# Gate and up products of a mixture-of-experts layer: two quarters of weights per change between fp32r and bf16 products

## The chip, the cores and the metric

The kernel runs on one core of a Trainium2 chip. The metric is the device time of one execution in microseconds (us). TensorE appears in the profile as PE (matmuls) and PEld (weight loads), VectorE as DVE, ScalarE as ACT, GpSimd as POOL and the DMA queue that loads weights as SP.

## The reference, cut to what matters

One encoder layer is applied to 512 prompt tokens and 1024 sample tokens. The part that the change touches is the expert layer: each of 16 experts takes its best 64 prompt and 128 sample tokens, 192 columns in all.

```python
def expert_choice_moe(h, w_router, w_gate, w_up, w_down):
    ...
    gates, idx = lax.top_k(probs.T, cap)
    xe = jnp.take(t, idx, axis=0)
    a = jnp.einsum("ecd,edf->ecf", xe, w_gate)
    b = jnp.einsum("ecd,edf->ecf", xe, w_up)
    ye = jnp.einsum("ecf,efd->ecd", jax.nn.silu(a) * b, w_down)
    ye = ye * gates[..., None].astype(ye.dtype)
    out = jnp.zeros_like(t).at[idx.reshape(-1)].add(ye.reshape(-1, D))
```

The widths are 1024 for a token, 2048 for an expert's inner layer. All arrays are fp32.

## The kernel before, in words

Every fp32 weight is used as a sum of a rounded fp32r part (`wh`, made by ACT in `split_hi`, L937) and a bf16 remainder (`wl`, made by DVE in `split_lo`, L946). Tokens too are kept as a high part, its remainder and a bf16 copy.

The weights of an expert come in six units of 4 MB: gate and up of the first half of the inner layer, gate and up of the second half, and two halves of down. Each unit is worked in four quarters; `QS` lists all quarters in order and `qi` counts them. A quarter of gate or up is 256 inner columns, that is two blocks of 128 (`f`) by eight blocks of depth (`k`). One expert therefore has 16 quarters of gate and up (4 g, 4 u, 4 g, 4 u) and 8 of down.

`gu_mm` (L1172) does one quarter on PE: 16 fp32r products of 384 columns (L1180, the tokens and their remainder side by side), and then 16 bf16 products of 192 columns (L1184), which add the weights' remainder to the first 192 columns. Both sum into one PSUM tile `pg`. The pool `psG` has two buffers of it, which are four of the eight PSUM banks; `S` and `Pp` of the down products hold the other four.

`gu_out` (L1238) takes the tile out of PSUM: ACT copies the remainder's columns into `t` (L1243) and DVE adds the others to it (L1244), and after that `pg` is free. A gate quarter then gets a sigmoid on ACT (L1250) and a product on DVE into `sil` (L1251). An up quarter gets a product with `sil` on DVE (L1255) and is split into the operand `hT` of the down products: two ACT copies (L1263, L1266) and two DVE subtractions (L1264, L1265). `t` and `sg` have two buffers each (pool `ev`).

Every engine runs its own instructions in the order in which they are written, and waits by semaphores for the others. The order is written out in the loop over `qi`: the products of quarter `qi` come first, then `gu_out` of the quarter before it, and inside that, at the call `between()`, the weight splits for later quarters: `split_hi(qi + 3)` on ACT and `split_lo(qi + 2)` on DVE. `wh` has four buffers and `wl` six. When the last quarter of a unit is split, `load` issues the DMA of the unit after the next into the raw buffer that came free (two buffers).

Of the kernel before, what the change touches and what calls it, by code (L numbers as in the profile page):

```python
# [6 lines left out]
F32 = mybir.dt.float32  # L7
F32R = mybir.dt.float32r
BF16 = mybir.dt.bfloat16
I32 = mybir.dt.int32  # L10
U32 = mybir.dt.uint32
AF = mybir.ActivationFunctionType
# [5 lines left out]
P = 128  # L18
D = 1024
KD = D // P  # L20
# [6 lines left out]
KF = FE // P  # L27
# [8 lines left out]
def encoder(ctx: ExitStack, tc, xp, xs_, pp, ps_, norm1_g, w_in, conv_k, conv_b, ln_g, ln_b, pool_w,  # L36
            pool_scale, w_out, norm2_g, w_router, w_gate, w_up, w_down, w_ple, w_pg, b_pg, final_g,
            yp, ys):
    nc = tc.nc
# [28 lines left out]
    def rpool(name, bufs, st=None):  # L68
        return (st or rgt).enter_context(tc.tile_pool(name=name, bufs=bufs, side="right"))
# [11 lines left out]
    for g in range(4):  # L81
        h = 1 << g
# [674 lines left out]
    def own(e):  # L757

        return (0, CP, 0) if e % 2 == 0 else (CP, 0, CS)
# [51 lines left out]
    for it in range(24):  # L811
        b, r = divmod(it, 8)
        c, h = divmod(r, 2)
# [93 lines left out]
    NQ = len(QS)  # L907
    RAW, HL = {}, {}

    def load(u, pieces=range(4)):  # L910
        if u >= NU:
            return
        down = units[u][1:3] == ("d", NE - 1)
        if 0 in pieces:
            RAW[u] = rawp.tile([P, KF, 512] if down else [P, KD, D], F32, name="raw")
        step = 4 if down else 2
        src = units[u][0].rearrange("(k p) n -> p k n", p=P)
        for q in pieces:
            c = slice(q * step, (q + 1) * step)
            nc.sync.dma_start(RAW[u][:, c, :], src[:, c, :])  # L920

    def split_hi(qi):
        if qi >= NQ:
            return
        u, q = QS[qi]
        raw = RAW[u]
        if units[u][1] in "gu":
            src = raw[:, :, q * 256:(q + 1) * 256]
            shape = [P, KD, 256]
        elif units[u][1:3] == ("d", NE - 1):  # L930
            src = raw[:, 4 * q:4 * q + 4, :]
            shape = [P, 4, 512]
        else:
            src = raw[:, 2 * q:2 * q + 2, :]
            shape = [P, 2, D]
        h = hlp.tile(shape, F32R, name="wh")
        nc.scalar.activation(h, src, AF.Copy)  # L937
        HL[qi] = (h, src, shape)

    def split_lo(qi):  # L940
        if qi >= NQ:
            return
        u, q = QS[qi]
        h, src, shape = HL[qi]
        l = hlp2.tile(shape, BF16, name="wl")
        nc.vector.tensor_sub(l, src, h.bitcast(F32))  # L946
        HL[qi] = (h, l)
        if q == 3:
            RAW.pop(u)
            load(u + 2)  # L950
# [115 lines left out]
    for i in range(12):  # L1066
        a = 4 * i
        at(a + 1, x1_half, i, 0)
        at(a + 3, x1_half, i, 1)
        t = max(a + 2, OB + 2 * i)  # L1070
# [91 lines left out]
    with ExitStack() as sc:  # L1162
        hep = rpool("he", 1, sc)
        ev = rpool("ev", 2, sc)
        ev1 = rpool("ev1", 1, sc)
        ps_g = sc.enter_context(tc.tile_pool(name="psG", bufs=2, space=PSUM))
        ps_d = sc.enter_context(tc.tile_pool(name="psD", bufs=1, space=PSUM))

        hT = None
        sil = None  # L1170
        S = Pp = None

        def gu_mm(e, qi):
            h, l = HL.pop(qi)
            xT, xb = XT[e]
            pg = ps_g.tile([P, 2, 512], F32, name="pg")
            c = slice(own(e)[0], own(e)[0] + 192)
            for f in range(2):
                for k in range(KD):
                    nc.tensor.matmul(pg[:, f, 0:384].rearrange("p (a t) -> p a t", a=2), h[:, k, f * P:(f + 1) * P],  # L1180
                                     xT[:, k, :, c], start=(k == 0), stop=False)
            for f in range(2):
                for k in range(KD):
                    nc.tensor.matmul(pg[:, f, 0:192], l[:, k, f * P:(f + 1) * P], xb[:, k, c],  # L1184
                                     start=False, stop=(k == KD - 1))
            return pg

        WL = []

# [44 lines left out]
                                             start=False, stop=True, skip_group_check=True)  # L1234
                WL.clear()

        LA = 3
        def gu_out(kind, e, hf, q, pg, between):  # L1238

            nonlocal hT, sil  # L1240
            f0 = 8 * hf + 2 * q
            t = ev.tile([P, 2, 192], F32, name="t")
            nc.scalar.activation(t, pg[:, :, 192:384], AF.Copy)  # L1243
            nc.vector.tensor_add(t, pg[:, :, 0:192], t)  # L1244
            sg = ev.tile([P, 2, 192], F32, name="sg")
            if kind == "g":
                between()
                if q == 0:
                    sil = ev1.tile([P, KD, 192], F32, name="sil")
                nc.scalar.activation(sg, t, AF.Sigmoid)  # L1250
                nc.vector.tensor_mul(sil[:, 2 * q:2 * q + 2, :], t, sg)  # L1251
            else:
                if hf == 0 and q == 0:
                    hT = (hep.tile([P, KF, 384], F32R, name="hT"), hep.tile([P, KF, 192], BF16, name="hTb"))
                nc.vector.tensor_mul(sg, t, sil[:, 2 * q:2 * q + 2, :])  # L1255
                last = hf == 1 and q == 3
                if not last:
                    between()
                hh = hT[0][:, f0:f0 + 2, :]

                _, so, po = own(e)
                a, b = (64, 0) if e % 2 == 0 else (0, 192)
                nc.scalar.activation(hh[:, :, a:a + 192], sg, AF.Copy)  # L1263
                nc.vector.tensor_sub(hh[:, :, 256:384], sg[:, :, so:so + CS], hh[:, :, a + so:a + so + CS].bitcast(F32))  # L1264
                nc.vector.tensor_sub(hh[:, :, b:b + CP], sg[:, :, po:po + CP], hh[:, :, a + po:a + po + CP].bitcast(F32))  # L1265
                nc.scalar.activation(hT[1][:, f0:f0 + 2, :], sg, AF.Copy)  # L1266
                if last:
                    between()

        YT = []  # L1270

        def down_out(e, hf, q, between):

            between()
            if q < 3 or hf == 0 and e < NE - 1:
                return
            if hf == 0 or e < NE - 1:
                YE[0] = ev1.tile([P, D], F32, name="ye_s")
                YE[1] = ev1.tile([CP, D], F32, name="ye_p")
            cs = (0, 1) if e < NE - 1 else (hf,)  # L1280
            for n in cs:
                nc.scalar.activation(YE[0][:, n * 512:(n + 1) * 512], S[:, n, :], AF.Copy, scale=gt_s[:, e:e + 1])  # L1282
            for n in cs:
                t = ev1.tile([CP, 512], F32, name="yt")
                nc.scalar.activation(t, Pp[CP:, n, :], AF.Copy, scale=gt_p[CP:, e:e + 1])
                nc.vector.scalar_tensor_tensor(YE[1][:, n * 512:(n + 1) * 512], Pp[:CP, n, :], gt_p[:CP, e:e + 1], t,  # L1286
                                               op0=OP.mult, op1=OP.add)
            c = slice(cs[0] * 512, (cs[-1] + 1) * 512)
            for g, src, ix in (("s", YE[0], idx_s[:, e:e + 1]), ("p", YE[1], idx_p[:CP, e:e + 1])):
                nc.gpsimd.indirect_dma_start(out=acc_d[g], out_offset=bass.IndirectOffsetOnAxis(ap=ix, axis=0),  # L1290
                                             in_=src[:, c], in_offset=None, element_offset=c.start,
                                             compute_op=OP.add)

        YE = {}
        late = None
        for qi in range(NQ - 4):
            u, q = QS[qi]
            _, kind, e, hf = units[u]
            nxt = None
            between = lambda: (split_hi(qi + LA), split_lo(qi + LA - 1)) if qi < NQ - 5 else None  # L1300
            if kind == "d" and hf == 0 and q == 0:
                late(between)
                late = None
            if kind in "gu":
                pg = gu_mm(e, qi)
                nxt = lambda f, a=(kind, e, hf, q, pg): gu_out(*a, f)
            elif kind == "d":
                if qi == NQ - 5:
                    pt = ps_g.tile([P, 2, 512], F32, name="pg")
                    pt = pt.rearrange("p i (k t) -> p i k t", k=4)  # L1310
                    for f in (t_T, t_split):
                        for i in range(2):
                            f(i, 0, pt[:, i])
                down_mm(e, hf, q, qi)
                nxt = lambda f, a=(e, hf, q): down_out(*a, f)
            if late:
                late(between)
            elif not (kind == "d" and hf == 0 and q == 0):
                between()
            late = nxt  # L1320
            if qi == NQ - 6:
                rx = rawp.tile([P, KF, 512], F32, name="raw")
                for i in range(2):
                    x2_load(i, slice(0, 512))
            if kind == "d" and 1 <= 4 * hf + q <= 4:
                turn(e + 1, 4 * hf + q - 1, lambda: ps_g.tile([P, 2, 512], F32, name="pg"))
# [10 lines left out]
    with ExitStack() as sd:  # L1337
# [58 lines left out]
        for i in range(12):  # L1396
# [5 lines left out]
            for n in range(len(cuts) - 1):  # L1402
                c = slice(cuts[n], cuts[n + 1])
# [57 lines left out]
```

## Time and profile before

| | us |
|---|---|
| median of 3 runs (lowest to highest) | 2303.33 (2302.74 to 2307.52) |
| the profiled execution, its time | 2308.3 |
| its span, first to last instruction | 2306.5 |

The profile describes that one execution. Besides busy times it gives, for each group of instructions, the idle time of the engine just before them and the instruction that ended it. A chain view follows the work that ended last back through time, and a timeline shows each engine's instructions with start and length; runs of equal instructions are merged as x16 and the like. The ends of matmuls are modelled, and a matmul's length includes its way through the array, so that consecutive ones overlap: what counts is the distance of their starts.

### The profile page before, as it was taken

The page shows a single profiled execution, that of the slowest core. Times are in us where ns is not written, and L with a number is a line of the kernel's source. Part 1 is how long each engine was busy: PE and PEld are TensorE (multiplying, and loading weights), DVE is VectorE, ACT ScalarE, POOL GpSimd, SP SyncE. Part 2 cuts the span into 40 slices and gives each one's busy share as a digit, 9 for nine tenths or more (in the row PEclk, how much of TensorE's full clock was granted, in tenths as well). Part 3 has the DMA queues.
Part 4 walks back from the last instruction along what each step waited for, and adds up shares of the span by engine and source line. Part 5 has one row for each costly group of instructions (what it writes and reads, how often), then busy time and mean ns, then how long its engine had stood idle before and what let it go on. Part 6 is the DMA issues. An engine that isn't in the chain of part 4 may idle for free.

```text
span 2306.5 us, 36990 instructions
## 1 busy us (share of the span) xinstructions
PE 2243.6 (97%) x15062; PEld 1912.3 (83%) x15106; DVE 1734.4 (75%) x2320; ACT 1404.2 (61%) x1837; POOL 277.0 (12%) x538
## 2 busy tenths in 40 slices
PE   7999889988999999999999999999999999999997
PEld 6888777768898979889798988979788898988675
DVE  8898763576877878787787878778787877878565
ACT  4324336546767667676676767667676766666443
POOL 0122232221001010100101010010101001000322
PEclk9999999999999999999999999999999999999999
DMA  6434555547687686767767676876767677777442
GB/s 194 109 118 122 165 163 174 196 169 289 246 292 259 254 293 245 282 243 296 253 259 285 254 280 243 297 246 261 282 262 271 251 292 246 273 249 272 144 138 101
DMA packets 168874, 534.26 MB, mean 232 GB/s; under 512 B 11969, under 2 KB 38625, under 8 KB 168704
## 3 DMA queue, kind: packets, MB, share of 16 engines
q1 hardware_dynamic: 156064, 493.70, 58.5%
q0 software_dynamic: 9040, 31.46, 5.5%
q10 hardware_dynamic: 3600, 6.74, 0.8%
q8 instruction: 118, 1.93, 0.3%
q14 instruction: 52, 0.43, 0.1%
HBM read 481.34 MB, written 50.52 MB: 231 GB/s over the span
## 4 chain that ended last, share of the span: by engine, by line
PE 78%; issue 10%; DMA 4%; DVE 4%; ACT 2%; POOL 1%; SPq 0%; ACTq 0%; DVEq 0%; POOLq 0%
PE pg L1180 27%; PE pg L1184 13%; PE S L1217 9%; PE Pp L1217 4%; PE S L1227 4%; PE Pp L1233 2%; PE pz L103 2%; PE pz L104 2%; PE pz L105 2%; PE po L1369 2%; PE po L1370 2%; PE po L1372 2%; PE pz L413 2%; DMA acc_s<-ye_s,idx_s 1%; PE pz L606 1%
## 5 line engine op out<-in xcount | busy, mean ns | idle before, releaser
L946 DVE TENSOR_TENSOR wl<-raw,wh 128x2048 bf16<-128x2048 f32 x388 | 881.7, 2283 | 65.6 <-issue 54.9
L1180 PE MATMUL pg<-xTe,wh 128*128 128x384 f32 x4096 | 777.3, 341 | 2.7 <-ACT wp L997 2.7
L937 ACT ACTIVATE wh<-raw 128x2048 fp32r<-128x2048 f32 x388 | 736.1, 1909 | 38.4 <-DMA raw<-in_w_up_dram 20.2
L1180 PEld LDWEIGHTS pg<-xTe,wh 128*128 128x128 f32 x4096 | 701.5, 188 | 9.3 <-ACT ye_s L1282 6.2
L1184 PE MATMUL pg<-xTb,wl 128*128 128x192 bf16 x4096 | 382.8, 247 | 0.0
L1184 PEld LDWEIGHTS <-wl 128*128 128x128 bf16 x4096 | 325.2, 98 | 40.3 <-issue 40.3
L1243 ACT ACTIVATE t<-pg 128x384 f32<-128x384 f32 x256 | 125.9, 492 | 300.4 <-PE pg L1184 299.7
L1217 PE MATMUL S<-wh,hT 128*128 128x512 f32 x1024 | 285.4, 398 | 0.6 <-ACT ye_s L1282 0.6
L1244 DVE TENSOR_TENSOR t<-pg,t 128x384 f32<-128x384 f32 x256 | 142.7, 557 | 158.7 <-ACT t L1243 157.9
L1217 PEld LDWEIGHTS S<-wh,hT 128*128 128x128 f32 x1024 | 186.4, 188 | 36.7 <-ACT ye_s L1282 1.0
L103 PE MATMUL pz<-xTh,wb 128*128 128x256 f32 x576 | 167.0, 290 | 0.7 <-ACT xTh L212 0.5
L104 PE MATMUL pz<-xTl,wb 128*128 128x256 f32 x576 | 164.4, 285 | 1.5 <-DVE xTl L213 1.5
L105 PE MATMUL pz<-xTh,wb 128*128 128x256 f32 x576 | 164.2, 285 | 0.0
L746 POOL DMA_INDIRECT xg_s<-h_s,idx_s x16 | 24.2, 1513 | 1159.1 <-PE pg L778 579.1
L1217 PE MATMUL Pp<-wh,hT 128*128 128x512 f32 x512 | 160.9, 390 | 0.8 <-DVE ye_p L1286 0.8
L429 DVE SCALAR_TENSOR_TENSOR acc<-u,kT,acc 128x496 f32<-128x496 f32 (+2 forms) x168 | 126.8, 755 | 5.1
L103 PEld LDWEIGHTS pz<-xTh,wb 128*128 128x128 f32 x576 | 111.8, 194 | 10.8 <-issue 5.8
L1217 PEld LDWEIGHTS Pp<-wh,hT 128*128 128x128 f32 x512 | 96.1, 188 | 22.3 <-DVE ye_p L1286 1.2
L782 DVE SCALAR_TENSOR_TENSOR xTe<-pg,vT,xTe 128x128 fp32r<-128x128 f32 (+1 forms) x120 | 49.5, 412 | 86.0 <-ACT xTe L781 83.9
L104 PEld LDWEIGHTS pz<-xTl,wb 128*128 128x128 f32 x576 | 111.9, 194 | 1.9 <-DVE xTl L213 1.7
L105 PEld LDWEIGHTS pz<-xTh,wb 128*128 128x128 f32 x576 | 111.9, 194 | 0.0
L1227 PE MATMUL S<-wl,hTb 128*128 128x512 bf16 x480 | 108.8, 379 | 2.2
(290 smaller groups left out, 2661.0 us busy)
## 6 DMA issues: line engine op xcount, KB each, us to landing
raw<-in_w_gate_dram SPq DMA_DIRECT2D x128, 1024.0 KB, 6.4
raw<-in_w_up_dram SPq DMA_DIRECT2D x128, 1024.0 KB, 8.4
raw<-in_w_down_dram SPq DMA_DIRECT2D x128, 1024.0 KB, 6.3
u<-u_d SPq DMA_DIRECT2D x32, 262.0 KB, 5.5
st<-yT_d SPq DMA_DIRECT2D x12, 512.0 KB, 5.6
ple_d<-wp SPq DMA_DIRECT2D x12, 512.0 KB, 8.9
pl<-ple_d SPq DMA_DIRECT2D x12, 512.0 KB, 4.7
out_dram<-raw SPq DMA_DIRECT2D x11, 512.0 KB, 2.9
```

Of the source, the lines that this page charges most:

```text
L103: nc.tensor.matmul(out, wh, xh, start=first, stop=False)
L104: nc.tensor.matmul(out, wh, xl, start=False, stop=False)
L105: nc.tensor.matmul(out, wl, xh, start=False, stop=last)
L429: nc.vector.scalar_tensor_tensor(acc[:, :n], u[:, s:s + n], kT[:, c, s:s + 1], acc[:, :n], op0=OP.mult, op1=OP.add)
L937: nc.scalar.activation(h, src, AF.Copy)
L946: nc.vector.tensor_sub(l, src, h.bitcast(F32))
L1180: nc.tensor.matmul(pg[:, f, 0:384].rearrange("p (a t) -> p a t", a=2), h[:, k, f * P:(f + 1) * P], xT[:, k, :, c], start=(k == 0), stop=False)
L1184: nc.tensor.matmul(pg[:, f, 0:192], l[:, k, f * P:(f + 1) * P], xb[:, k, c], start=False, stop=(k == KD - 1))
L1217: nc.tensor.matmul(out[:, n, :], x, rhs(h, i, n), start=(k == 0 and first), stop=(out is Pp and k == KF - 1))
L1227: nc.tensor.matmul(S[:, n, :], hT[1][:, k, so:so + CS], rhs(l, i, n), start=False, stop=(k == KF - 1))
L1243: nc.scalar.activation(t, pg[:, :, 192:384], AF.Copy)
L1244: nc.vector.tensor_add(t, pg[:, :, 0:192], t)
```

## The change

Gate and up are worked in pairs of quarters. `gu_mm` takes two `pg` tiles, does the 32 fp32r products of both quarters and then the 32 bf16 products of both. `gu_out` evicts both tiles, and does the rest for both, with one call of `between()` in the pair. The splits are handed out by two counters (`NXT`) instead of fixed offsets: at a gate or up pair that begins at quarter `qi`, both kinds are brought up to quarter `qi + 3`, that is two of each; down quarters do as before. The pools are as before, so a pair takes both `pg` buffers, both `t` and both `sg`.

```diff
         def gu_mm(e, qi):
-            h, l = HL.pop(qi)
+            hl = [HL.pop(qi + i) for i in range(2)]
             xT, xb = XT[e]
-            pg = ps_g.tile([P, 2, 512], F32, name="pg")
+            pgs = [ps_g.tile([P, 2, 512], F32, name="pg") for _ in range(2)]
...
+            for pg, (h, _) in zip(pgs, hl):
+                for f in range(2):
+                    for k in range(KD):
+                        nc.tensor.matmul(pg[:, f, 0:384].rearrange("p (a t) -> p a t", a=2),
+                                         h[:, k, f * P:(f + 1) * P], xT[:, k, :, c], start=(k == 0), stop=False)
+            for pg, (_, l) in zip(pgs, hl):
+                for f in range(2):
+                    for k in range(KD):
+                        nc.tensor.matmul(pg[:, f, 0:192], l[:, k, f * P:(f + 1) * P], xb[:, k, c],
+                                         start=False, stop=(k == KD - 1))
+            return pgs
...
-        def gu_out(kind, e, hf, q, pg, between):
+        def gu_out(kind, e, hf, q, pgs, between):
...
+            ts = []
+            for pg in pgs:
+                t = ev.tile([P, 2, 192], F32, name="t")
+                nc.scalar.activation(t, pg[:, :, 192:384], AF.Copy)
+                nc.vector.tensor_add(t, pg[:, :, 0:192], t)
+                ts.append(t)
+            sgs = [ev.tile([P, 2, 192], F32, name="sg") for _ in range(2)]
             if kind == "g":
                 between()
...
+                for i in range(2):
+                    nc.scalar.activation(sgs[i], ts[i], AF.Sigmoid)
+                    nc.vector.tensor_mul(sil[:, 2 * (q + i):2 * (q + i) + 2, :], ts[i], sgs[i])
+                return
...
+            for i in range(2):
+                nc.vector.tensor_mul(sgs[i], ts[i], sil[:, 2 * (q + i):2 * (q + i) + 2, :])
+            last = hf == 1 and q == 2
+            if not last:
+                between()
...
+        NXT = {"hi": 3, "lo": 2}
+        def splits(hi, lo):
+            for key, f, n in (("hi", split_hi, hi), ("lo", split_lo, lo)):
+                while NXT[key] <= min(n, NQ - 3 - (key == "lo")):
+                    f(NXT[key])
+                    NXT[key] += 1
+
         for qi in range(NQ - 4):
...
+            if kind in "gu" and q % 2:
+                continue
             nxt = None
-            between = lambda: (split_hi(qi + LA), split_lo(qi + LA - 1)) if qi < NQ - 5 else None
+            z = qi + (kind in "gu")
+            between = lambda: splits(z + 3 - (kind in "gu"), z + 2) if qi < NQ - 5 else None
```

On PE, at the first two changes of quarters of expert 0, the order before is this; `wl` is the bf16 remainder of the weights, and the 16 loads and products of a quarter are cut after the first.

```order
L1180 MATMUL pg<-xTe,wh 128x384 x16
L1184 LDWEIGHTS wl
L1184 MATMUL pg<-xTb,wl 128x192
...
L1180 MATMUL pg<-xTe,wh 128x384 [waits DVE_49]
L1180 MATMUL pg<-xTe,wh 128x384 x15
L1184 LDWEIGHTS wl
```

At the same place of the changed kernel, the beginning of the second pair, it is this.

```order
L1187 MATMUL pg<-xTb,wl 128x192
L1182 MATMUL pg<-xTe,wh 128x384 [waits DVE_49]
L1182 MATMUL pg<-xTe,wh 128x384 x15
L1182 MATMUL pg<-xTe,wh 128x384 [waits DVE_49]
L1182 MATMUL pg<-xTe,wh 128x384 x15
L1187 LDWEIGHTS wl
```

The wait for DVE's addition of an older tile stands ahead of each tile's first product in both; the tile waited for was the one before last, with a whole quarter of products behind it, and is now the first of the pair just ended.

On DVE, in gate quarters and then an up quarter of an expert, the order before is this: addition, a weight split, product, quarter by quarter.

```order
L1244 TENSOR_TENSOR t<-pg,t 128x384 [waits Activation_49]
L946 TENSOR_TENSOR wl<-raw,wh 128x2048
L1251 TENSOR_TENSOR sil<-t,sg 128x384 [waits Activation_49]
L1244 TENSOR_TENSOR t<-pg,t 128x384 [waits Activation_49]
L1255 TENSOR_TENSOR sg<-t,sil 128x384 [waits DVE_49]
L946 TENSOR_TENSOR wl<-raw,wh 128x2048
L1264 TENSOR_TENSOR hT<-sg,hT 128x2x128 [waits DMASW7_49,DMASW2_49,Activation_49]
L1265 TENSOR_TENSOR hT<-sg,hT 128x2x64
```

In the changed kernel the same stretch, the second gate pair and an up pair, is this.

```order
L1247 TENSOR_TENSOR t<-pg,t 128x384 [waits Activation_49] x2
L946 TENSOR_TENSOR wl<-raw,wh 128x2048 [waits Activation_49] x2
L1256 TENSOR_TENSOR sil<-t,sg 128x384 [waits Activation_49] x2
L1247 TENSOR_TENSOR t<-pg,t 128x384 [waits Activation_49] x2
L1261 TENSOR_TENSOR sg<-t,sil 128x384 [waits DVE_49] x2
L946 TENSOR_TENSOR wl<-raw,wh 128x2048 [waits Activation_49] x2
L1272 TENSOR_TENSOR hT<-sg,hT 128x2x128 [waits Activation_49]
L1273 TENSOR_TENSOR hT<-sg,hT 128x2x64
```

The remainder splits `wl` now wait for ACT, which they did not before: the high part that they need is made in the same pair and not one quarter earlier.

On ACT, in the same gate quarters, the order before is the first of the next two pieces, and that of the changed kernel the second.

```order
L1243 ACTIVATE t<-pg 128x384 [waits PE_49,Activation_49]
L937 ACTIVATE wh<-raw 128x2048
L1250 ACTIVATE sg<-t 128x384 [waits DVE_49]
L1243 ACTIVATE t<-pg 128x384 [waits PE_49,Activation_49]
L937 ACTIVATE wh<-raw 128x2048
```

```order
L1246 ACTIVATE t<-pg 128x384 [waits DVE_49,PE_49] x2
L937 ACTIVATE wh<-raw 128x2048 x2
L1255 ACTIVATE sg<-t 128x384 [waits DVE_49] x2
L1246 ACTIVATE t<-pg 128x384 [waits DVE_49,PE_49] x2
L937 ACTIVATE wh<-raw 128x2048 [waits DMAHW2_49,DMAHW7_49,DMAHW1_49,DMAHW0_49]
L937 ACTIVATE wh<-raw 128x2048
```

The first copy of a pair out of PSUM now waits for DVE as well as for PE: it writes into the buffer `t` that the product of the gate pair before it reads.

## Rows read from the trace of the kernel before

**Rows 1.** The page: the span, and PE's busy time with its share.

```profile
span 2306.5 us, 36990 instructions
PE 2243.6 (97%) x15062; PEld 1912.3 (83%) x15106; DVE 1734.4 (75%) x2320; ACT 1404.2 (61%) x1837; POOL 277.0 (12%) x538
```

**Rows 2.** The chain that ended last, one gate quarter: start, us, what.

```profile
1158.14 2.81 PE pg L1180 x16
1160.95 1.33 PE pg L1184 x16
```

**Rows 3.** Windows: length, busy PE, PEld, DVE, ACT, POOL, PEclk, DMA.

```profile
1170.58:1203.75 33.17, 33.17 (x257) 31.91 (x257) 28.32 (x33) 23.41 (x28) 0.00 (x0) 1.00 0.67 254
2130.00:2150.00 20.00, 17.45 (x86) 11.44 (x85) 8.82 (x6) 7.68 (x9) 6.61 (x2) 1.00 0.56 179
```

**Rows 4.** Timelines of PE alone, short windows in one gate quarter: start, length.

```profile
1191.10 0.60 PE L1180 MATMUL pg<-xTe,wh 128*128 128x384 f32 x2
...
1193.96 1.50 PE L1184 MATMUL pg<-xTb,wl 128*128 128x192 bf16 x16
```

**Rows 5.** The page's groups: busy us, mean ns of one, idle before.

```profile
L1184 PE MATMUL pg<-xTb,wl 128*128 128x192 bf16 x4096 | 382.8, 247 | 0.0
...
L1243 ACT ACTIVATE t<-pg 128x384 f32<-128x384 f32 x256 | 125.9, 492 | 300.4 <-PE pg L1184 299.7
```

**Rows 6.** Timeline, an eviction in a gate quarter and one among up quarters.

```profile
1195.24 3.03 PE L1180 MATMUL pg<-xTe,wh 128*128 128x384 f32 x16
1195.56 0.49 ACT L1243 ACTIVATE t<-pg 128x384 f32<-128x384 f32 x1 [1.44 <-PE pg L1184]
1195.94 1.91 ACT L937 ACTIVATE wh<-raw 128x2048 fp32r<-128x2048 f32 x1
1196.08 0.56 DVE L1244 TENSOR_TENSOR t<-pg,t 128x384 f32<-128x384 f32 x1 [0.92 <-ACT t L1243]
...
1198.75 0.55 DVE L1251 TENSOR_TENSOR sil<-t,sg 128x384 f32<-128x384 f32 x1
...
1203.50 0.42 DVE L1264 TENSOR_TENSOR hT<-sg,hT 128x256 fp32r<-128x256 f32 x1
...
1203.83 0.28 DVE L1265 TENSOR_TENSOR hT<-sg,hT 128x128 fp32r<-128x128 f32 x1
...
1206.40 1.50 PE L1184 MATMUL pg<-xTb,wl 128*128 128x192 bf16 x16
...
1207.94 0.49 ACT L1243 ACTIVATE t<-pg 128x384 f32<-128x384 f32 x1 [0.97 <-PE pg L1184]
```

**Rows 7.** Timelines of ACT and DVE, splits back to back.

```profile
1214.64 3.70 ACT L937 ACTIVATE wh<-raw 128x2048 fp32r<-128x2048 f32 x2
...
1214.69 0.28 DVE L1265 TENSOR_TENSOR hT<-sg,hT 128x128 fp32r<-128x128 f32 x1
1214.89 4.49 DVE L946 TENSOR_TENSOR wl<-raw,wh 128x2048 bf16<-128x2048 f32 x2
```

**Rows 8.** Timeline, two places where PE waited for another engine.

```profile
540.26 0.62 PE L1180 MATMUL pg<-xTe,wh 128*128 128x384 f32 x2 [2.68 <-ACT wp L997]
...
2137.56 0.74 DVE L1286 SCALAR_TENSOR_TENSOR ye_p<-Pp,gt_p,yt 64x512 f32<-64x512 f32 x1 [3.09 <-ACT yt L1285]
...
2138.36 0.50 PE L1217 MATMUL Pp<-wh,hT 128*128 128x512 f32 x1 [0.75 <-DVE ye_p L1286]
```

**Rows 9.** Timelines, the change from up to down and the next expert's first addition.

```profile
1211.83 1.18 PE L1217 MATMUL S<-wh,hT 128*128 128x512 f32 x4
...
1212.08 0.49 ACT L1243 ACTIVATE t<-pg 128x384 f32<-128x384 f32 x1 [1.03 <-PE pg L1184]
...
1250.57 0.56 DVE L1244 TENSOR_TENSOR t<-pg,t 128x384 f32<-128x384 f32 x1 [1.63 <-ACT t L1243]
```

**Rows 10.** The chain that ended last, the third down quarter's first products.

```profile
1217.77 0.92 PE S L1217 x4
```

More of the change, by code (lines that the diff above doesn't have):

```diff
@@ L1173, in gu_mm @@
         def gu_mm(e, qi):
-            h, l = HL.pop(qi)
+            hl = [HL.pop(qi + i) for i in range(2)]
             xT, xb = XT[e]
-            pg = ps_g.tile([P, 2, 512], F32, name="pg")
+            pgs = [ps_g.tile([P, 2, 512], F32, name="pg") for _ in range(2)]
             c = slice(own(e)[0], own(e)[0] + 192)
[L1178 to L1186, printed above, removed]
+            for pg, (h, _) in zip(pgs, hl):
[9 more added lines that the diff above has]
+            return pgs
         WL = []
@@ L1235, in down_mm @@
                 WL.clear()
-        LA = 3
-        def gu_out(kind, e, hf, q, pg, between):
+        def gu_out(kind, e, hf, q, pgs, between):
             nonlocal hT, sil
[L1241 to L1245, printed above, removed]
+            ts = []
[5 more added lines that the diff above has]
+            sgs = [ev.tile([P, 2, 192], F32, name="sg") for _ in range(2)]
             if kind == "g":
@@ L1249, in gu_out @@
                     sil = ev1.tile([P, KD, 192], F32, name="sil")
[L1250 to L1258, printed above, removed]
+                for i in range(2):
+                    nc.scalar.activation(sgs[i], ts[i], AF.Sigmoid)
+                    nc.vector.tensor_mul(sil[:, 2 * (q + i):2 * (q + i) + 2, :], ts[i], sgs[i])
+                return
+            if hf == 0 and q == 0:
+                hT = (hep.tile([P, KF, 384], F32R, name="hT"), hep.tile([P, KF, 192], BF16, name="hTb"))
+            for i in range(2):
[3 more added lines that the diff above has]
+                between()
+            _, so, po = own(e)
+            a, b = (64, 0) if e % 2 == 0 else (0, 192)
+            for i, sg in enumerate(sgs):
+                f0 = 8 * hf + 2 * (q + i)
                 hh = hT[0][:, f0:f0 + 2, :]
-                _, so, po = own(e)
-                a, b = (64, 0) if e % 2 == 0 else (0, 192)
                 nc.scalar.activation(hh[:, :, a:a + 192], sg, AF.Copy)
@@ L1266, in gu_out @@
                 nc.scalar.activation(hT[1][:, f0:f0 + 2, :], sg, AF.Copy)
-                if last:
-                    between()
+            if last:
+                between()
         YT = []
@@ L1304, in encoder @@
             if kind in "gu":
-                pg = gu_mm(e, qi)
-                nxt = lambda f, a=(kind, e, hf, q, pg): gu_out(*a, f)
+                nxt = lambda f, a=(kind, e, hf, q, gu_mm(e, qi)): gu_out(*a, f)
             elif kind == "d":
```

## The prediction

> **What bounds the kernel now.** Read the page first: PE is busy for 2243.6 us of a span of 2306.5 [rows 1]. Then the chain that ended last, through a stretch of gate and up: it consists of PE alone, quarter after quarter, 2.81 us of fp32r products and 1.33 us of bf16 ones [rows 2]. The windows confirm it: in eight quarters PE is busy for 33.17 of 33.17 us, at a granted clock of 1.00 (the higher level, 2.4 GHz), while DVE has 28.32 and ACT 23.41 [rows 3]. So a quarter costs 33.17 / 8 = 4.146 us, set by PE's own pace, and nothing is waited for. ACT idles ahead of its copies out of PSUM, 300.4 us over 256 of them, for PE's products [rows 5]. The reader is to see two things: PE can only get faster by what is lost inside its own stream, and every wait put into that stream is paid in full. DVE is not the bound, but with 28.32 of 33.17 it has only 0.6 us to spare per quarter.
>
> **What the change takes away.** What is lost at a change of kind shows as the difference between the quarter and its steady pace. A run of 16 fp32r products lasts 3.03 us [rows 6] and its first two last 0.60 [rows 4]: 2.43 / 14 = 0.174 us from one to the next. A run of 16 bf16 products lasts 1.50 us [rows 4], the last of them 0.25 [rows 5]: 1.25 / 15 = 0.083. Sixteen of each are 4.10 us; 0.05 of the 4.146 belongs to one change there and one back. 256 quarters become 128 pairs, and 128 × 0.05 = **6.4 us** is all that can be won (0.28%). A pair then wants 2 × 4.146 − 0.05 = 8.24 us.
>
> **What it adds: an eviction on PE's path.** A pair fills both `pg` tiles, so the first product of the next pair waits for the addition on the first tile of the pair just done. Before, a whole quarter lay between; now only the second tile's bf16 run does. Count from the end of the first tile's bf16 run. The second run takes 16 × 0.083 = 1.32, and the next fp32r run starts 0.22 before the end of a bf16 run (1195.24 against 1193.96 + 1.50 [rows 4, 6]), so PE wants the tile at 1.10. The eviction: ACT starts 0.10 after the run's end where its copy also waits for a buffer `t` that a gate product used (1195.56 against 1195.46 [rows 4, 6]) and 0.04 where it doesn't (1207.94 against 1207.90 [rows 6]); the copy takes 0.49, DVE follows 0.03 later and takes 0.56 [rows 6]; PE follows DVE by 0.06 (2138.36 against 2137.56 + 0.74 [rows 8]). Together 1.24 or 1.18: PE is **late by 0.14 or 0.08 with ACT and DVE idle**. After a wait the first two fp32r products last 0.62 [rows 8] and not 0.60 [rows 4], so 0.02 more: 0.16 or 0.10 a boundary, already more than the 0.05 saved.
>
> The trace analysis page of the Trainium skill (Perfetto Trace Analysis, "Matmuls" under "Optimizing Tensor Performance") asks that independent matmul groups rotate through PSUM banks, so that one group's evacuation overlaps the next group's matmuls. The rows of before agree (33.17 busy of 33.17); by that rule the change would lay open all of an eviction at a boundary, some 1.2 us, while by the rows 1.10 of it stay covered by the second tile's own bf16 run, and the sum goes by the rows.
>
> **What it adds: DVE comes late as well.** The pair's work on DVE is no more than before, but its order has a new hole: `wl` now waits for the `wh` of the same pair. After a pair (same zero): ACT copies the second tile at 1.32 + 0.10 = 1.42 (or 1.36), begins the first split 0.38 later [rows 6], at 1.80, and ends it 1.91 later [rows 6], at 3.71; DVE begins `wl` at 3.74, though its additions (and, in an up pair, its products) end long before. Two `wl` take 4.49, and the next operation starts 0.08 before the end (1214.69 + 0.28 against 1214.89 [rows 7]): 8.15. Then
> - gate pair: the first product ends 0.55 later [rows 6], at 8.70. Only then may ACT write that `t` again: 8.73, and DVE's next addition stands at 8.73 + 0.49 + 0.03 = 9.25 (9.19 where the pair began with 1.36);
> - up pair: four subtractions, twice 0.33 + 0.20 (starts 1203.50 and 1203.83 [rows 6], 1214.69 and 1214.89 [rows 7]): 8.15 + 1.07 = 9.22 (9.16).
>
> The addition would like to start at 0.62 or 0.56 of the next pair's own zero, which lies 8.24 plus the wait after this one. Walking through the seven boundaries of an expert (pairs g g u u g g u u):
> 1. first addition in time: 0.10, next zero at 8.34;
> 2. DVE free at 9.19 − 8.34 = 0.85 instead of 0.62: 0.16 + 0.23 = 0.39, next zero 8.63;
> 3. 9.25 − 8.63 = 0.62, in time: 0.16, next 8.40;
> 4. 9.22 − 8.40 = 0.82 instead of 0.56: 0.10 + 0.26 = 0.36, next 8.60;
> 5. 9.16 − 8.60 = 0.56, in time: 0.10;
> 6. like 2: 0.39;
> 7. like 3: 0.16.
>
> A long wait gives DVE the time that it lacked, so long and short alternate: 1.66 us an expert, which is 0.24 a boundary. Less 8 × 0.05 = 0.40 that the changes save: 1.26 × 16 experts = **20.2 us**.
>
> **Costed at nothing.** The last pair of an expert is followed by down products in other banks; no wait. There, ACT evicts and splits `hT` first and only then makes `wh` for the third down quarter. It starts its second copy 0.25 after the down products begin [rows 9], reaches that split some 3.2 us later (two copies' hand-over to DVE, a product, four copies) and ends it at about 5.4; it is needed at 1217.77 − 1211.83 = 5.94 [rows 9, 10]. If that cover of 0.5 were gone, each further 0.1 would cost 1.6 us in all. The first pair of an expert gets one more `wl` ahead of its addition, 2.2 us, where DVE idled 1.63 us [rows 9] and where the addition now comes a further fp32r run (2.8 us) later: covered by 2.2. DMA: the last `wl` of a gate or up unit ends slightly earlier than before, relative to PE, and the first `wh` of the unit after the next is asked for later, so loads have more time. SP and POOL keep their order.
>
> **Rivals.**
> *A, every boundary late.* If hand-overs among ACT, DVE and PE cost about 0.3 us more per pair than the rows above, DVE is late at each boundary and short waits vanish: 7 × 0.39 − 0.40 = 2.33, times 16 = 37 us, **2340.6**. For it: the walk rests on rounded single rows, and the 28.32 of 33.17 leaves little slack. Against: each row repeats in every quarter.
> *B, the latency alone.* If DVE reaches its next addition 0.25 sooner than worked out, only the bare 0.10 and 0.16 stay: 3 × 0.10 + 4 × 0.16 − 0.40 = 0.54, times 16 = 9 us, **2312**. Against: the `wl` behind the `wh` is in the order itself.
> *C, it doesn't show.* Waits of 0.06 a boundary pay for the saving: **2303**, no change. It needs B and a release faster by 0.07.
> *D, faster.* The one mechanism: PE's first product of a pair really needs the bank later than its recorded start, its weight load coming first, and additions end in time; then no wait replaces the changes saved: −6.4 us, **2296.9**. It decides where the waits of an expert sum to less than 0.1 us. Against: PE's record where it waited shows weight load and product both after the release [rows 8].
> *E, the clock falls.* Waits at every boundary could cost PE its higher clock. At 1.2 GHz a pair takes 8.24 us more; one pair in each expert would be 132 us, **2435**. Against: in 2130 to 2150 PE is busy for only 17.45 of 20 us, with a wait of 0.75 among others, and the granted clock stays at 1.00 [rows 3, 8]. The page TensorE: Matmul & The Clock Gate of the Trainium skill ("A second HAM failure mode: psum-queue depth-cycling") has this as a rule: micro-idles of PE between groups that cycle through PSUM make the clock oscillate. By that rule this rival would be likely; the trace of before, with its few waits, does not bear it out.
>
> **How the numbers follow.** The sum is made on the profiled execution, 2306.5 + 20.2 = 2326.7 us of span; that execution's time, 2308.3, lies 5.0 above the median of the runs, and the difference is put on the median: 2303.3 + 20.2 = **2323.5**. Chances: forecast 0.58 (its own range 2315 to 2333), A 0.15, B 0.12, C 0.06, D 0.07, E 0.02. The range **2305 to 2342** leaves out D, half of C, E and the far end of A. What a measurement of this kernel can tell from no change is about 0.2%, 4.6 us: slower 0.87 (forecast, A, B, E), same 0.06, faster 0.07.
>
> **What would show it.** In the profile after: PE's fp32r group has idle time released by DVE's addition, about 7 × 16 = 112 times and 1.66 × 16 − 112 × 0.02, some 24 us in all, long and short in turn, the longest near 0.4 us; fp32r runs of 32; a `wl` that waits for ACT's `wh` in every pair; no wait at the start of a down half; a clock of 1.00 throughout gate and up. Wrong would be: no idle time of PE there (D), even waits (A or B), waits for DMA or at the third down quarter, or a stretch at half the clock.

## The result, and the profile after

The changed kernel takes 2328.86 us (median of 4 runs, 2324.73 to 2331.90), the kernel before 2304.55 (4 runs on both occasions together); the ratio is 1.0100, with a 95% interval of 1.0087 to 1.0114. It is slower by 24.3 us, where 20.2 were forecast. The profiled execution lasts 2331.27.

The page of the changed kernel answers [rows 1] and [rows 5] so: span, engines, and the groups of the low split, the fp32r products with their weight loads, and the copy out of PSUM.

```profile
span 2329.5 us, 37020 instructions
PE 2257.5 (97%) x15062; PEld 1929.8 (83%) x15106; DVE 1732.0 (74%) x2320; ACT 1401.5 (60%) x1837; POOL 276.7 (12%) x538
...
L946 DVE TENSOR_TENSOR wl<-raw,wh 128x2048 bf16<-128x2048 f32 x388 | 873.5, 2287 | 184.6 <-ACT wh L937 140.4 <-issue 44.2
L1182 PE MATMUL pg<-xTe,wh 128*128 128x384 f32 x4096 | 746.6, 338 | 12.7 <-DVE t L1247 9.2 <-ACT wp L997 1.7
L1182 PEld LDWEIGHTS pg<-xTe,wh 128*128 128x128 f32 x4096 | 705.7, 188 | 35.7 <-DVE t L1247 22.2 <-ACT ye_s L1290 6.2 <-ACT wp L997 2.1
L1247 DVE TENSOR_TENSOR t<-pg,t 128x384 f32<-128x384 f32 x256 | 142.6, 557 | 121.8 <-ACT t L1246 115.9
L1246 ACT ACTIVATE t<-pg 128x384 f32<-128x384 f32 x256 | 125.7, 491 | 357.3 <-PE pg L1187 279.8 <-DVE sil L1256 77.4
```

Three releases here are new or have grown: DVE's low split waits 140.4 us for ACT's high split (10.7 before), ACT's copy waits 77.4 us for DVE's gate product, and PE's products and loads wait for DVE's addition. PE's share of busy time is still 97%, and that is the page's trap in this case: the modelled end of a bf16 run lies 0.22 us past the point where the next fp32r run can start (1195.46 against 1195.24 [rows 4, 6]), so the first 0.22 us of a wait leave no idle time in the record. One reads the distance of the starts instead. The timeline of PE alone, the eight pairs of one expert and the first down product:

```profile
1150.28 5.82 PE L1182 MATMUL pg<-xTe,wh 128*128 128x384 f32 x32
1155.94 2.81 PE L1187 MATMUL pg<-xTb,wl 128*128 128x192 bf16 x32
1158.61 5.83 PE L1182 MATMUL pg<-xTe,wh 128*128 128x384 f32 x32
1164.28 2.81 PE L1187 MATMUL pg<-xTb,wl 128*128 128x192 bf16 x32
1167.45 5.84 PE L1182 MATMUL pg<-xTe,wh 128*128 128x384 f32 x32 [0.36 <-DVE t L1247]
1173.14 2.81 PE L1187 MATMUL pg<-xTb,wl 128*128 128x192 bf16 x32
1175.80 5.83 PE L1182 MATMUL pg<-xTe,wh 128*128 128x384 f32 x32
...
1184.41 5.84 PE L1182 MATMUL pg<-xTe,wh 128*128 128x384 f32 x32
...
1192.77 5.82 PE L1182 MATMUL pg<-xTe,wh 128*128 128x384 f32 x32
...
1201.46 5.84 PE L1182 MATMUL pg<-xTe,wh 128*128 128x384 f32 x32 [0.22 <-DVE t L1247]
...
1209.82 5.82 PE L1182 MATMUL pg<-xTe,wh 128*128 128x384 f32 x32
...
1218.07 1.18 PE L1220 MATMUL S<-wh,hT 128*128 128x512 f32 x4
```

From pair to pair it is 8.33, 8.84, 8.35, 8.61, 8.36, 8.69 and 8.36 us: short and long in turn, as the walk in the prediction had it. From the first gate product to the first down product it is 1218.07 − 1150.28 = 67.79 us. This **stretch** is the measure for all that follows; before the change it is 66.37, sixteen quarters of 4.146 and the fractions at either end. Over the profiled executions the 16 stretches are longer by 21.6 us (1085.0 against 1063.4; the first stretch before the change was itself 1.6 us longer than its others, for a reason told under the sum below). The down halves are the same to 0.04 us in all.

What makes an addition late is seen where ACT and DVE stand at the longest of these waits, the one that ends at 1167.45:

```profile
1158.80 0.49 ACT L1246 ACTIVATE t<-pg 128x384 f32<-128x384 f32 x1 [0.83 <-PE pg L1187]
1159.31 3.72 ACT L937 ACTIVATE wh<-raw 128x2048 fp32r<-128x2048 f32 x2
1159.32 0.56 DVE L1247 TENSOR_TENSOR t<-pg,t 128x384 f32<-128x384 f32 x1 [0.76 <-ACT t L1246]
1161.26 4.49 DVE L946 TENSOR_TENSOR wl<-raw,wh 128x2048 bf16<-128x2048 f32 x2 [1.39 <-ACT wh L937]
...
1165.67 1.02 DVE L1256 TENSOR_TENSOR sil<-t,sg 128x384 f32<-128x384 f32 x2
1166.32 0.49 ACT L1246 ACTIVATE t<-pg 128x384 f32<-128x384 f32 x1 [2.46 <-DVE sil L1256]
1166.84 0.56 DVE L1247 TENSOR_TENSOR t<-pg,t 128x384 f32<-128x384 f32 x1
```

PE's run for that tile ended at 1164.28 + 1.50 = 1165.78; the copy that follows it starts 0.54 us later, held by DVE's gate product, which is held by two low splits, which waited 1.39 us for the high split.

### The profile page after: what moved, and what is told of

Read it like the earlier page. It is cut to its first block, busy times and chain, and to the rows that moved or that the text cites. A ratio compares the mean times of both kernels' runs of the same rounds, so it can differ in the third digit from the quotient of the medians.

```text
span 2329.5 us, 37020 instructions
## 1 busy us (share of the span) xinstructions
PE 2257.5 (97%) x15062; PEld 1929.8 (83%) x15106; DVE 1732.0 (74%) x2320; ACT 1401.5 (60%) x1837; POOL 276.7 (12%) x538
## 4 chain that ended last, share of the span: by engine, by line
PE 66%; DVE 14%; ACT 8%; issue 7%; DMA 3%; POOL 1%; SPq 0%; ACTq 0%; DVEq 0%; POOLq 0%
PE pg L1182 19%; PE S L1220 10%; PE pg L1187 9%; DVE wl L946 7%; ACT wh L937 5%; PE Pp L1220 5%; PE S L1230 4%; PE Pp L1236 2%; PE po L1388 2%; PE po L1389 2%; PE pz L103 2%; PE po L1391 2%; PE pz L104 2%; PE pz L105 2%; PE pz L413 2%
## 5 line engine op out<-in xcount | busy, mean ns | idle before, releaser
L946 DVE TENSOR_TENSOR wl<-raw,wh 128x2048 bf16<-128x2048 f32 x388 | 873.5, 2287 | 184.6 <-ACT wh L937 140.4
L1182 PE MATMUL pg<-xTe,wh 128*128 128x384 f32 x4096 | 746.6, 338 | 12.7 <-DVE t L1247 9.2
L1182 PEld LDWEIGHTS pg<-xTe,wh 128*128 128x128 f32 x4096 | 705.7, 188 | 35.7 <-DVE t L1247 22.2
L937 ACT ACTIVATE wh<-raw 128x2048 fp32r<-128x2048 f32 x388 | 720.8, 1905 | 15.0 <-DMA raw<-in_w_gate_dram 8.0
L1187 PE MATMUL pg<-xTb,wl 128*128 128x192 bf16 x4096 | 360.3, 246 | 0.0
L1187 PEld LDWEIGHTS <-wl 128*128 128x128 bf16 x4096 | 331.6, 98 | 20.1 <-issue 17.8
L1246 ACT ACTIVATE t<-pg 128x384 f32<-128x384 f32 x256 | 125.7, 491 | 357.3 <-PE pg L1187 279.8
L1230 PEld LDWEIGHTS <-hTb 128*128 128x128 bf16 x512 | 47.5, 98 | 61.3 <-issue 8.4
```

What stands on the lines that cost most here:

```text
L1230: nc.tensor.matmul(S[:, n, :], hT[1][:, k, so:so + CS], rhs(l, i, n), start=False, stop=(k == KF - 1))
```

## The experiments

All stand beside runs of the kernel before on the same chip: 2304.55 is its median beside the change, 2304.97 beside e1 to e4 and 2305.09 beside e5 and e6. The stretch is the median of the 16 experts' stretches, read from PE's timeline.

| | us, median | ratio (95% interval) | stretch, us |
|---|---|---|---|
| before | 2304.97 | | 66.37 |
| the change | 2328.86 | 1.0100 (1.0087 to 1.0114) | 67.81 |
| e1, low split from an older high part | 2307.77 | 1.0014 (1.0005 to 1.0023) | 66.61 |
| e2, a high split between the copies | 2314.06 | 1.0044 (1.0029 to 1.0059) | 66.94 |
| e3, quarters on PE, pairs elsewhere | 2331.15 | 1.0110 (1.0095 to 1.0126) | 67.97 |
| e4, lent banks | 2296.80 | 0.9967 (0.9955 to 0.9979) | 65.94 |
| e5, lent banks, quarters on PE | 2305.05 | 0.9997 (0.9988 to 1.0006) | 66.37 |
| e6, t read once | 2320.73 | 1.0069 (1.0054 to 1.0085) | 67.43 |

The theory is that of the prediction: PE waits at each pair's end for an eviction that begins late, because DVE's low splits wait for high splits of the same pair. Its rival: the loss comes with PE's own order, which goes through both PSUM tiles and returns at once, or from too much work for ACT and DVE at one place.

**e1, the hole in DVE's order taken away.**

```diff
-        nc.vector.tensor_sub(l, src, h.bitcast(F32))
+        old = OLD.get("h")
+        same = old is not None and list(old[1]) == list(shape) and units[u][1] in "gu"
+        nc.vector.tensor_sub(l, src, (old[0] if same else h).bitcast(F32))
+        OLD["h"] = (h, shape)
```

> The changed kernel, but in gate and up the low part of a quarter's weights is the weights minus the high part of the quarter before it, so that DVE never waits for a high part made in the same pair; all operations, sizes and loads stay, the output is not the reference's. Theory (DVE comes late because its low split waits for ACT's high split of the same pair): the long waits at boundaries 2, 4 and 6 of an expert fall to the bare eviction, 0.10 to 0.16 us each; 3 x 0.10 + 4 x 0.16 - 0.40 = 0.54 us an expert, 9 us over the kernel before: 2313. Rival (DVE is late because paired evictions are simply too much work in one place, or PE pays for the change of bank by itself): the waits stay long and the time stays at 2329.

It went further than expected. The second low split of a pair still reads a high part of its own pair, but the first one of the two, which is done by then. In its timelines of PE and DVE (L1185 are the fp32r products, L948 the low splits, L1250 the additions) the pairs follow each other evenly, and DVE's low splits stand directly behind the additions:

```profile
1140.24 5.82 PE L1185 MATMUL pg<-xTe,wh 128*128 128x384 f32 x32
...
1148.57 5.83 PE L1185 MATMUL pg<-xTe,wh 128*128 128x384 f32 x32
...
1156.90 5.83 PE L1185 MATMUL pg<-xTe,wh 128*128 128x384 f32 x32
```

```profile
1149.27 0.56 DVE L1250 TENSOR_TENSOR t<-pg,t 128x384 f32<-128x384 f32 x1 [0.76 <-ACT t L1249]
1149.75 4.48 DVE L948 TENSOR_TENSOR wl<-raw,wh 128x2048 bf16<-128x2048 f32 x2
1154.15 1.02 DVE L1259 TENSOR_TENSOR sil<-t,sg 128x384 f32<-128x384 f32 x2
1156.29 0.56 DVE L1250 TENSOR_TENSOR t<-pg,t 128x384 f32<-128x384 f32 x1 [1.12 <-ACT t L1249]
```

All boundaries now take 8.33, so the bare eviction costs 8.33 − 8.24 = 0.09 us, behind gate pairs too, where 0.16 had been worked out. DVE has 1.12 us to spare, with the same operations as in the change: too much work it is not. 21 of the 24 us go away with this one dependence.

**e2, one of two high splits between the two copies** (gate pairs only; the counters are handed over in two calls).

```diff
                 nc.scalar.activation(t, pg[:, :, 192:384], AF.Copy)
+                if not ts and kind == "g":
+                    between(1)
                 nc.vector.tensor_add(t, pg[:, :, 0:192], t)
```

> The changed kernel, but in gate pairs ACT makes one of its two high splits between the copies of the first and the second tile, not behind both. Theory: that high part is ready at 2.3 us of the pair and not at 3.7, so DVE's low splits start 0.5 us earlier, right behind its second addition, and the buffer t comes free before the next pair wants it. Boundaries 2 and 6 (behind gate pairs) fall from 0.60 and 0.47 to about 0.16, boundary 4 (behind an up pair) stays near 0.36: 0.44 + 0.30 us less an expert, 12 us in all: 2317. Rival (the bank, not DVE's order): no change, 2329.

The stretch fell by 0.87 us, of 0.74 expected. The boundaries of an expert are 8.33, 8.36, 8.33, 8.60, 8.36, 8.35, 8.34: the two behind gate pairs are nearly bare, and the one behind an up pair, whose order is as it was, keeps 0.36.

```profile
1152.03 5.82 PE L1182 MATMUL pg<-xTe,wh 128*128 128x384 f32 x32
...
1160.39 5.82 PE L1182 MATMUL pg<-xTe,wh 128*128 128x384 f32 x32
...
1168.72 5.84 PE L1182 MATMUL pg<-xTe,wh 128*128 128x384 f32 x32
...
1177.33 5.82 PE L1182 MATMUL pg<-xTe,wh 128*128 128x384 f32 x32
```

So order alone, with nothing left out, gives back 15 of the 24 us.

**e3, PE's order of before with paired evictions and splits.**

```diff
-            for pg, (h, _) in zip(pgs, hl):
+            for pg, (h, l) in zip(pgs, hl):
                 for f in range(2):
...
-            for pg, (_, l) in zip(pgs, hl):
                 for f in range(2):
```

> The changed kernel with PE's own order as before the change: 16 fp32r and 16 bf16 products for one tile and then for the other; evictions and splits stay in pairs. Nothing is saved at changes of kind. Theory (lateness comes from the paired evictions and splits on ACT and DVE): the second tile ends 4.15 us behind the first, the high split behind its copy ends at 6.5, two low splits at 11.0, the products of a gate pair at 11.5, and the next addition starts at 12.1, where PE, which wants the tile 3.93 after the next zero (8.29), needs it to start by 11.6: late by 0.5 at every other boundary, 3 x 0.5 us an expert, 24 us: 2328. Rival (what costs is that PE runs through both banks and comes back with only one bf16 run between): no waits at all, 2304.6.

2331.15 is 3 us above the theory's number, and the rival's is 26.6 us away. Its timeline of PE shows the wait at every other boundary, although PE now has a whole quarter between, and its page names DVE's product behind ACT's copies (L1245, L1246 and L1255 are copy, addition and gate product):

```profile
857.91 3.03 PE L1182 MATMUL pg<-xTe,wh 128*128 128x384 f32 x16
860.78 1.50 PE L1186 MATMUL pg<-xTb,wl 128*128 128x192 bf16 x16
862.68 3.07 PE L1182 MATMUL pg<-xTe,wh 128*128 128x384 f32 x16 [0.40 <-DVE t L1246]
```

```profile
L1245 ACT ACTIVATE t<-pg 128x384 f32<-128x384 f32 x256 | 125.3, 489 | 365.2 <-PE pg L1186 206.8 <-DVE sil L1255 156.8 <-DMA ple_d<-wp 1.2
```

The quarter from 857.91 to 862.68 is 4.77 long, 0.62 over 4.146. So PE's new order is not needed for the loss; pairs on ACT and DVE alone bring it.

**e4, lent banks.** The two tiles of the down products, idle during gate and up, serve every other pair.

```diff
-            pgs = [ps_g.tile([P, 2, 512], F32, name="pg") for _ in range(2)]
+            n = qi % 24 // 2
+            g = lambda: ps_g.tile([P, 2, 512], F32, name="pg")
+            d = lambda name: ps_d.tile([P, 2, 512], F32, name=name)
+            pgs = [g(), g()] if n in (0, 2, 4, 6) else [d("S"), d("Pp")] if n < 7 else [d("Pp"), g()]
```

> The changed kernel with four more PSUM banks for gate and up: the two tiles that the down products use are lent to the second, fourth and sixth pair of each expert, and one of them to the first quarter of the eighth pair. Nothing else is changed; ACT and DVE stay as late as they are. Theory (the loss is PE's wait for the eviction of the pair just done): no boundary waits, since a whole pair lies between, and what is left is the saving of 8 x 0.05 us an expert, 6.4 us: 2298, faster than the kernel before. Rival (ACT and DVE have too little time for a pair's work, and PE meets them later): the waits come back elsewhere, at the first products of down or at weights not yet split, and the time stays above 2304.6.

2296.80, faster than both kernels. Its window over six pairs, the timeline of PE in it and the page's row of the low splits:

```profile
1146.50:1195.98 49.48, 49.48 (x389) 48.54 (x386) 40.83 (x45) 34.22 (x40) 0.00 (x0) 1.00 0.66 248
```

```profile
1146.54 3.02 PE L1185 MATMUL S<-xTe,wh 128*128 128x384 f32 x16
...
1154.78 5.80 PE L1185 MATMUL pg<-xTe,wh 128*128 128x384 f32 x32
...
1163.02 3.02 PE L1185 MATMUL S<-xTe,wh 128*128 128x384 f32 x16
```

```profile
L946 DVE TENSOR_TENSOR wl<-raw,wh 128x2048 bf16<-128x2048 f32 x388 | 873.3, 2287 | 184.4 <-ACT wh L937 140.1 <-issue 44.3
```

Pairs are 8.24 us apart, what the prediction gave a pair without waits. DVE is as late as in the change (140.1 us of waiting for the high split, against 140.4), and nobody waits for it.

**e5, lent banks with PE's order of before** (the edits of e4 and e3 together).

> The kernel with the lent banks, but PE does 16 fp32r and 16 bf16 products for one tile and then for the other, as before the change. Theory (the gain with lent banks is the halved number of changes of kind, 0.427 us an expert by the gate and up stretch of 65.94 against 66.37 us): with no boundary waits and all changes back, the stretch is 66.37 again and the time that of the kernel before, 2305. Rival (the lent banks win something else, waits of before that the trace doesn't show): it stays at 2297.

2305.05 and a stretch of 66.37, those of before; from pair to pair it is 8.29 again.

```profile
1156.38 3.03 PE L1185 MATMUL pg<-xTe,wh 128*128 128x384 f32 x16
...
1164.67 3.03 PE L1185 MATMUL S<-xTe,wh 128*128 128x384 f32 x16
```

So e4 owes its gain to the halved changes of kind: 66.37 − 65.94 = 0.43 us an expert, 6.8 in all; the medians of e4 and e5 are 8.3 apart, with runs that spread over 6.0 and 4.2.

**e6, the buffer t without DVE as its last reader.**

```diff
-                    nc.vector.tensor_mul(sil[:, 2 * (q + i):2 * (q + i) + 2, :], ts[i], sgs[i])
+                    nc.vector.tensor_mul(sil[:, 2 * (q + i):2 * (q + i) + 2, :], sgs[i], sgs[i])
```

> The changed kernel, but the product of a gate pair on DVE multiplies the sigmoid with itself instead of with t, so that the last reader of t is ACT itself and its copy of the next pair never waits for DVE; the output is not the reference's. It separates the two causes of DVE's lateness, the low split's wait for the high split and the buffer t. Theory (both count, the split far more): behind gate pairs the next addition moves from 1.17 us after the first product's start to 0.96, so boundaries 2 and 6 fall by 0.21 us each, 0.42 an expert, 7 us in all: 2322. Rival (the buffer t is the main cause): boundaries 2 and 6 fall to the bare 0.09, 0.9 us an expert, 14 us or more: 2314.

DVE's next addition follows the first gate product (L1256) by 0.94 us, and not by 1.17:

```profile
1159.57 1.02 DVE L1256 TENSOR_TENSOR sil<-sg 128x384 f32<-128x384 f32 x2
1160.51 0.55 DVE L1247 TENSOR_TENSOR t<-pg,t 128x384 f32<-128x384 f32 x1
```

Boundaries 2 and 6 fell to 8.60 and 8.46, by 0.24 each, and 3 and 7 rose by 0.06, since a shorter wait hands part of the lateness on. Boundary 2 in PE's timeline:

```profile
1152.51 5.82 PE L1182 MATMUL pg<-xTe,wh 128*128 128x384 f32 x32
...
1161.11 5.82 PE L1182 MATMUL pg<-xTe,wh 128*128 128x384 f32 x32
```

The stretch is 0.38 shorter, 6.1 us in all, where 7 were expected; the medians are 8.1 apart. Both causes are real: the buffer is worth about a quarter of the loss, and removing the low split's wait (e1) takes the buffer's share along, since the gate product then ends in time.

## Why the prediction was right

**The saving.** Forecast 0.05 us a pair, 6.4 in all. e4 against e5 shows 8.24 against 8.293, 0.053 a pair, 6.8 in all. Right.

**PE's wait, with ACT and DVE idle.** Forecast 0.10 or 0.16 a boundary; e1 measures 0.09 at all seven. The step that was off is the 0.10 taken for ACT's start behind a gate pair, from 1195.56 against 1195.46 [rows 4, 6]. In the changed kernel the copy at 1174.67 starts 0.03 after the run's end, though it waits for DVE and PE (the run that it follows ended at 1173.14 + 1.50):

```profile
1174.67 0.49 ACT L1246 ACTIVATE t<-pg 128x384 f32<-128x384 f32 x1 [2.62 <-PE pg L1187]
```

So the 0.10 is not the price of a second wait as such. The order lists hold the difference: the copy of before names PE's semaphore first and ACT's own second, the copy of the change DVE's first and PE's second. In both traces the copy starts about 0.10 behind the event where the one named first comes last (1195.56 behind 1195.46; 1166.32 behind the gate product's end at 1166.22), and in the changed kernel 0.03 where the one named second does. Nearly all such copies of the two traces agree, but no run changed that order alone. The mis-sized term is why rival B, at 2312, priced the bare eviction 4 us too high: e1 gives 2307.8.

**DVE late, and in turn.** Forecast boundaries 0.10, 0.39, 0.16, 0.36, 0.10, 0.39, 0.16, together 1.66; over the 8.24 of a pair the profile has 0.09, 0.60, 0.11, 0.37, 0.12, 0.45, 0.12, together 1.86. The alternation stands, and e1, e2 and e6 show its cause. Boundary 2 was mis-sized, by 0.21; that the bare eviction had been priced 0.09 too high at boundaries 3 and 7 together hid part of it, by luck. Two terms in its chain were: ACT began its first split 0.51 after the second copy, not 0.38 (1158.80 and 1159.31), and the next copy began 0.10 after the gate product's end, not 0.03 (1165.67 + 0.55 and 1166.32). The second is in boundary 6 too (0.45 for 0.39). The 0.51 could have been read before: the first split after the first copy of an expert has it in the trace of before as well, and the walk took its 0.38 from a later quarter.

```profile
1250.05 0.49 ACT L1243 ACTIVATE t<-pg 128x384 f32<-128x384 f32 x1 [1.88 <-PE pg L1184]
1250.57 1.92 ACT L937 ACTIVATE wh<-raw 128x2048 fp32r<-128x2048 f32 x1
```

That split is the first of a new 4 MB unit, which waits for that unit's loads; but so are those ahead of boundaries 4 and 6, and they begin 0.38 after their copies (1175.99 and 1176.37, 1192.95 and 1193.33). Such waits alone do not explain the 0.13, and its cause stays open.

**What was costed at nothing.** The down halves last as long as before, to 0.04 us over fifteen experts, so the cover of 0.5 us ahead of the third down quarter held, and the first pair's of 2.2. No loads were waited for on PE in gate and up.

**The sum.** 1.26 × 16 = 20.2 us were forecast. The 21.6 by which the stretches differ in the profiled executions is not yet the price of the pairs. In the kernel before, PE's first gate run came after a wait of 2.68 us and ran in part at the lower of TensorE's two levels, half the clock, so the first expert's stretch took 67.93 us, 1.6 more than the other fifteen. PE's timeline there, and the window around it with a granted clock of 0.83:

```profile
540.26 4.61 PE L1180 MATMUL pg<-xTe,wh 128*128 128x384 f32 x16 [2.68 <-ACT wp L997]
```

```profile
535.00:545.00 10.00, 7.32 (x34) 6.38 (x33) 4.14 (x6) 6.97 (x9) 2.36 (x4) 0.83 0.79 276
```

Against sixteen stretches of 66.37 the pairs cost 1085.0 − 1061.9 = 23.1 us, 2.9 more than forecast, and boundary 2 is the most of that. The spans differ by 23.0: beside the 21.6 of the stretches, gate and up began 2.2 us earlier (538.08 against 540.26 [rows 8]), and behind the last expert's gate and up 3.5 us were added, of which 2.1 are a longer wait of PE for a load of `acc_s` (3.3 us; 1.2 before), with 3.4 us at half the clock behind it (shown at the end). Those 3.5 are not the change's: in e1 to e4, which all have its pairs, that part is between 0.2 and 0.6 longer than before.

**The rivals.** A (each boundary late) is out, by the alternation. C and D needed waits below 0.06; they are 0.09 at least, but D's time, 2296.9, is what e4 reaches once the waits have gone. E, the falling clock, did not come: the window of 540 to 2100 us holds about 105 such waits and its granted clock is 1.00.

```profile
540.00:2100.00 1560.00, 1547.24 (x10444) 1354.14 (x10473) 1206.58 (x1250) 1056.60 (x1222) 106.36 (x51) 1.00 0.71 263
```

The prediction said that the trace of before, with its few waits, does not bear such a fall out; it holds one, behind the 2.68 us above, a far longer wait than those at boundaries. The page TensorE: Matmul & The Clock Gate of the Trainium skill ("A second HAM failure mode: psum-queue depth-cycling") tells of a kernel in which such idling between groups made the clock oscillate; with waits of 0.09 to 0.6 us every 8 us, this trace does not agree. Of the Trainium skill's page Perfetto Trace Analysis ("Matmuls") e4, at 2296.80 us against 2328.86, bears out the rule that groups should rotate through banks.

**What it said the profile would show.** The runs of 32, the waits for the high split and the clock came as said. The idle time of PE did not: 24 us in 112 pieces had been named, and the page shows 9.2 us for DVE's addition (33 pieces by the list of waits) and 22.2 for the weight loads. The waits were there, but the modelled ends cover them.

## What to carry to other kernels

Batching work to save a switch also batches what follows it: before pairing, lay the consumer's chain (copy, addition, release) against the one run that now covers it, and look in the instruction order for an operand that used to be made a step earlier and is now made in the same step. When a double buffer becomes one buffer for a pair, look for another stage's idle PSUM tiles. And read short waits of PE from the distance of starts, not from its idle time.

## What the runs showed of the hardware that was not expected

A change from 16 fp32r products to 16 bf16 ones and back costs PE 0.053 us (two quarters take 8.293 us in e5 and 8.240 in e4). A wait of 3.29 us for a DMA near the end of the changed kernel's profiled execution was followed by 3.4 us at half the clock (granted 0.54 over the window), the lower of TensorE's two levels, and in the kernel before the wait of 2.68 us ahead of the first gate product was followed by half the clock too. The wait of 1.71 us at that place in the changed kernel was not (its first run of 32 lasted 5.82 us, like the others), nor were the 105 or so of up to 0.6 us:

```profile
2158.00:2166.27 8.27, 5.11 (x22) 3.87 (x22) 4.17 (x2) 2.86 (x2) 5.17 (x2) 1.00 0.61 125
2166.27:2169.68 3.41, 3.28 (x12) 2.93 (x13) 0.69 (x1) 1.29 (x3) 0.00 (x0) 0.54 0.05 10
```
